# Where a two-layer trunk copies its residual into a bank, takes third chunks' features and spills its residual

## The chip, the cores and the metric

The kernel runs on one core of a Trainium2 chip. The metric is the device time of one launch in microseconds, the median of several runs. A core has five engines that are named in the profile: TensorE (PE, with its weight loads as PEld), VectorE (DVE), ScalarE (ACT), GpSimd (POOL) and SyncE (SP). Each engine takes its own instructions strictly in the order in which the program lists them, so an instruction that waits holds up all that stand behind it on its engine.

## The reference

The reference is a decoder trunk of two layers on 256 tokens of width 2048, in float32. Layer 0 (even) runs two mixers side by side on one input projection; layer 1 (odd) runs an mLSTM. Each layer ends with a gated embedding.

```python
for i in range(DEPTH):                      # DEPTH = 2
    hn = rmsnorm(h, e_norm[j] if i % 2 == 0 else o_norm[j])
    if i % 2 == 0:
        u = hn @ e_w_in[j]                  # HGRN2 and RG-LRU branches
        mix = concatenate([ya, yb]) @ e_w_out[j]
    else:
        u = hn @ o_w_in[j]                  # q, k, v, output gate, z, i and f gates
        mix = yc @ o_w_out[j]               # yc: normalised mLSTM output, gated
    h = h + mix
    pl = rmsnorm(p[i] @ ple_w[i], ple_norm[i])
    h = h + sigmoid(h @ ple_gate_w[i]) * pl
return rmsnorm(h, final_norm)
```

All weights are read once. The residual `h` is what the change's copy and spill are about: 256 tokens by 2048, 2 MB.

## The kernel before

**Numbers in two parts.** A float32 operand is split into a rounded high part and the low rest (`whi`, `wlo` for weights, `ahl` for activations), and a product is three matmuls: high by high, high by low, low by high. A weight tile of 128x1024 (512 KB) lands by SyncE's queue in one of five `raw` buffers. ScalarE casts it to `whi` (L136), VectorE makes `wlo` (L137). Both have four buffers. Two tiles make a *quarter*: 24 matmuls of 128x512 on TensorE (L208 to L210 or L232). So the weights that are cast run at most two quarters ahead of TensorE.

**Stages.** The program is a row of stages, each a product of 256x2048 by 2048x2048 in four output *chunks* of 512 columns: the inputs of layer 0, its output `eo`, the embedding's gate `g0`, queries and keys `oqk`, values `ov`, gates `oog` and `oz`, the output `oo`, the gate `g1`. In a stage, the first two chunks run interleaved (`project_two`): quarters in the order (0,0), (0,1), (1,0), (1,1), (0,2), (1,2), (0,3), (1,3), chunk and quarter. The quarters 2 need the activations that come from the *third* chunk of the stage before.

**Chunks to features.** A stage leaves its chunks token by row; the next stage needs them feature by row. `to_features` transposes blocks on VectorE into a tile `w` (L555), writes it to DRAM and reads it back in four DMAs that rearrange it into a tile `r` (`across`, L674 and L677, all issued by GpSimd), and then waits a number of steps, the *lag*, before it emits the instructions that read `r`: on ScalarE L563 with a gain, L571 without, and splits. The lanes are named `fe`, `fg` and `fo`, and the DRAM tensors `dfe`, `dfg`, `dfo` with the chunk's number. `features` does the same for queries and keys (`dqk`, L1194).

**Order.** Side work is written as Python generators in named lanes. `pump`, called in the middle of each quarter, advances every lane by one step; `drain` runs a lane to its end. A scheduler then orders the instructions of each engine by the program's order and by priorities (`high_priority`); `issue_after` keeps an instruction behind another one in that order.

**Seven products.** The last two chunks of a stage are computed with seven products for eight in a part of the matrix (`seven`). It holds four PSUM banks: A, F and B (`mm`) and E (`mx`). The product A (L232) is made first. ScalarE copies it to F (L335) and its negative to B (L336); then the product on E begins. In the stage `oo` alone, E begins with the residual of chunk 3, copied by ScalarE (L338, `home`), so that the sum needs no extra addition.

**The residual's way.** In layer 0 the residual lies in four tiles `hq` of 512 KB. After stage `g0` the four are written to DRAM (`dh`, L1150, GpSimd's queue), and in stage `oz` four DMAs bring them back (`home`, L1423).

Of the kernel before, what the change touches and what calls it, by code (L numbers as in the profile page):

```python
# [11 lines left out]
F32 = mybir.dt.float32  # L12
# [3 lines left out]
AF = mybir.ActivationFunctionType  # L16
# [3 lines left out]
P = 128  # L20
# [24 lines left out]
def trunk(ctx: ExitStack, tc: tile.TileContext, a, out):  # L45
    nc = tc.nc
    v, s, gp, te, sy = nc.vector, nc.scalar, nc.gpsimd, nc.tensor, nc.sync
# [10 lines left out]
    dr = ctx.enter_context(tc.tile_pool(name="dr", bufs=1, space=bass.MemoryType.DRAM))  # L58
# [4 lines left out]
    last = {}  # L63

    def start(lane, gen):
        lanes.setdefault(lane, []).append(gen)

    def step(lane):
        q = lanes.get(lane)
        while q:  # L70
            if next(q[0], lanes) is not lanes:
                return True
            q.pop(0)
        return False
# [8 lines left out]
    def drain(*which):  # L83
        for lane in which:
            while step(lane):
                pass
# [35 lines left out]
    def block(src, c, n):  # L122
        return src[c * P:(c + n) * P].rearrange("(p n) -> p n", p=P)
# [90 lines left out]
    def split_weights(r):  # L214

        hi, lo = (wp.tile([P, 1024], F32R, name=n, tag=n) for n in ("whi", "wlo"))
        with tc.high_priority(offset=400):
            last["act"] = s.copy(hi, r).ins  # L218
            last["dve"] = v.tensor_tensor(out=lo, in0=r, in1=hi.bitcast(F32), op=ALU.subtract).ins  # L219
        return hi, lo  # L220
# [62 lines left out]
    def seven(w, j, act, qs, kqs, room, part, home=None, order=None):  # L283

        def src(b, side, kq):
            return block(w[4 * (j + b) + kq], side * 1024, 1024)

        def load(tile_of, b, side):
            tiles = []
            for kq in kqs:  # L290
                t = tile_of()
                sy.dma_start(out=t, in_=src(b, side, kq))
                tiles.append(t)
            return tiles

        def ring():
            return wp.tile([P, 1024], F32, name="raw", tag="raw", bufs=5)

        def split(tiles):
            return [split_weights(t) for t in tiles]  # L300

        def add(x, y):
            with tc.high_priority(offset=400):
                for xi, yi in zip(x, y):
                    v.tensor_tensor(out=xi, in0=xi, in1=yi, op=ALU.add)

        def add_loaded(x):
            for xi, kq in zip(x, kqs):
                gp.dma_start(out=xi, in_=src(1, 0, kq), accum_op=ALU.add)

        def soon(out, in0, in1, op):
            with tc.high_priority(offset=450):
                v.tensor_tensor(out=out, in0=in0, in1=in1, op=op)

        def keep(out, bank):
            with tc.high_priority(offset=450):
                s.copy(out, bank)

        def quadrant(side, hf):
            return stationary(act, [2 * kq + side for kq in kqs], hf)  # L320

        def combo(n):
            return [[t for kq in kqs for t in qs[n, kq][x]] for x in range(2)]

        acc = len(kqs) == 2
        rest = [kq for kq in range(4) if kq not in kqs]
        E = px.tile([P, 512], F32, name="mx", tag="mx")
        A, F, B = (pm.tile([P, 512], F32, name="mm", tag="mm") for _ in range(3))
        b5, g = part(), part()
        X = load(room, 0, 0)  # L330
        product(A, quadrant(0, 0), split(X), True)
        if acc:
            add_loaded(X)
        with tc.high_priority(offset=450):
            s.copy(F, A)  # L335
            with tc.issue_after(s.activation(B, F, AF.Copy, scale=-1.0).ins):  # L336
                if home is not None:
                    s.copy(E, home)  # L338
        Y = load(room, 1, 1)
        product(E, combo(4), split(Y), home is None)  # L340
        W = X
        if not acc:
            W = load(ring, 1, 0)
            add(Y, W)
            add(W, X)
        rows = [list(rest), list(rest)]
        did = set()
        for op in order or ORDERS[len(kqs)]:
            if op in "ab":
                b = "ab".index(op)  # L350
                kq = rows[b].pop(0)
                plain(w, j + b, kq, act, ((A, F), (E, B))[b], end=not rows[b])
            elif op == "5":
                product(B, combo(1), split(W))
                add(X, Y)
                if acc:
                    add_loaded(Y)
                keep(b5, B)
            elif op == "6":
                product(B, combo(2), split(X))  # L360
                keep(g, B)
            elif op == "2":
                Z = load(ring, 0, 1)
                product(A, quadrant(1, 0), split(Z))
            elif op == "4":
                product(F, quadrant(1, 1), split(X))
            elif op == "7":
                product(B, combo(3), split(Y))
                soon(b5, B, b5, ALU.subtract)
            elif op == ".":  # L370
                pump()
            elif op == "A":
                yield 0, 0, A
            elif op == "F":
                soon(b5, F, b5, ALU.subtract)
                yield 0, 1, b5
            did.add(op)
            if op in "26" and {"2", "6"} <= did:
                add(X, Z)
        if home is None:  # L380
            soon(g, E, g, ALU.add)
            yield 1, 0, g
        else:
            soon(home, E, g, ALU.add)
            yield 1, 0, None
        yield 1, 1, B
# [163 lines left out]
    def to_features(h, c, act, gain, name, more=None):  # L550

        w = room("w")
        w5 = w.rearrange("p (j c h t) -> p h c j t", j=4, c=4, h=2)
        for hf in range(2):
            v.transpose(w5[:, hf], h[:, hf].rearrange("p (c j q) -> p c j q", c=4, j=4))  # L555
        r = room("r")
        yield from across(w, r, f"d{name}{c}", 6)
        r5 = r.rearrange("p (i c h t) -> p c h i t", i=4, c=4, h=2)
        for b in range(2):
            if gain:  # L560
                x = tp.tile([P, 512], F32, name="xr", tag="hn", bufs=3)
                for k in range(2):
                    s.activation(x[:, k * T:(k + 1) * T].rearrange("p (h i t) -> p h i t", h=2, i=4), r5[:, 2 * b + k],  # L563
                                 AF.Copy, scale=pc(gain, 4 * c + 2 * b + k))
                act[2 * c + b] = split_act(x, "h")
            else:
                hi, lo, both = act_pair()
                for k in range(2):
                    src = r5[:, 2 * b + k]
                    hk, lk = (x[:, k].rearrange("p (h i t) -> p h i t", h=2, i=4) for x in (hi, lo))  # L570
                    s.copy(hk, src)  # L571
                    v.tensor_tensor(out=lk, in0=src, in1=hk.bitcast(F32), op=ALU.subtract)
                act[2 * c + b] = (hi, lo, both)
        if more is not None:
            yield
            more(c, r5)
# [94 lines left out]
    def across(w, r, name, lag):  # L671

        d = dr.tile([P, 1024], F32, name=name)
        gp.dma_start(out=d, in_=w)  # L674
        to = r.rearrange("p (i n) -> p i n", i=4)
        for j in range(4):
            last["hop"] = gp.dma_start(out=to[32 * j:32 * j + 32],  # L677
                                       in_=d.rearrange("(i q) (j n) -> j q i n", i=4, j=4)[j]).ins
        for _ in range(lag):
            yield  # L680
# [413 lines left out]
    hq = []  # L1094
# [27 lines left out]
    act = out_proj(hq, mixed(), "fe")  # L1122
# [22 lines left out]

    acth = ple_gate(hq, two_and_seven(a["g0"], act, ready(act, "fe"), (e0, "q4", 2), in_e0), pls, rp0, hss0, "on", "fg", gate_sums)
    away = []
    for c in range(4):
        d = dr.tile([P, 2, 512], F32, name=f"dh{c}")
        gp.dma_start(out=d, in_=hq[c])  # L1150
        away.append(d)
    l0.close()


# [18 lines left out]
    with tc.tile_pool(name="m1", bufs=2) as m1:  # L1173
# [191 lines left out]
                start("mix", mix_norm())  # L1365
        y = {}
        held = []
        drain("combos")
        store_of = [hp.tile([P, 1024], F32, name="pr", tag="h") for _ in range(2)]
        turn = []  # L1370

# [31 lines left out]
        for jj in (0, 2):  # L1403
            us = [m1.tile([P, 2, 512], F32, name="u", tag="vt", bufs=6) for _ in range(2)]
            for b, hf, src in pair(a["oz"], jj, True):
# [3 lines left out]
                for i in range(2):  # L1409
                    c = hf * 8 + 2 * j + i  # L1410
# [5 lines left out]
        hq = []  # L1416
# [47 lines left out]
        act = out_proj(hq, two_and_seven(a["oo"], y, ready(y, "fm"), (m1, "vt", 6), in_m1, lambda: hq[3][:, 0]), "fo")  # L1464
# [67 lines left out]
        y, yh, t, r = (tp.tile([P, 1], F32, name=n, tag=n, bufs=2) for n in ("fy", "fyh", "ft", "fr"))  # L1532
# [22 lines left out]
        yh, t, r = (tp.tile([P, 1], F32, name=n, tag=n, bufs=2) for n in ("fyh", "ft", "fr"))  # L1555
# [131 lines left out]
```

## Time and profile before

| | us |
|---|---|
| median of three runs (1029.83 to 1030.67) | 1030.06 |
| the profiled execution | 1031.47 |
| span of the profiled execution, first to last instruction | 1029.7 |
| TensorE busy | 1014.8 |
| VectorE busy | 824.3 |
| ScalarE busy | 648.6 |
| GpSimd busy | 105.1 |

The mean granted TensorE clock was 0.995 of the full one. In the rows of a timeline stand the start and the length in us, the engine, the line, the operation, out<-in, the size and the count; in brackets the idle time of the engine before it, and what ended it. A row of waits gives who waited for whom, the sum in us, how often, and the longest. A DMA's row gives the tensor, the count, the size of each and the median time from issue to landing. Busy matmuls overlap: one is shown as 0.39 us long although the next starts 0.23 us later.

### The profile page before, as it was taken

Reading aid. Unit: us, or ns where it says so; the run is one execution under the profiler, and the core shown is the slowest. Engines: PE = TensorE matmul, PEld = TensorE weight load, DVE = VectorE, ACT = ScalarE, POOL = GpSimd, SP = SyncE. Lnnn points to the kernel's source line nnn. Section 1 sums busy time; section 2 is a strip of 40 time slices with the busy share of each in tenths; the row PEclk is TensorE's granted clock in tenths of the full one; section 3 lists DMA queues with packets and bytes.
Section 4 is the critical chain, followed back from the end, with each engine's and each line's share of the span. In section 5 each row is a group of like instructions: output and inputs, shape, how many; then the busy total and the mean of one; then the engine's idle time right before and its main releaser. Section 6 shows DMA issues by size and latency. Waiting matters only on the chain.

```text
span 1029.7 us, 14491 instructions
## 1 busy us (share of the span) xinstructions
PE 1014.8 (99%) x5170; PEld 842.2 (82%) x5170; DVE 824.3 (80%) x1208; ACT 648.6 (63%) x933; POOL 105.1 (10%) x190
## 2 busy tenths in 40 slices
PE   9999999999999999999999999999999999899996
PEld 7888888888888888888788888888888888788886
DVE  6867969969686888887659997778889997886684
ACT  7675554686874555565547866765667767454562
POOL 0111101011111112021011100000011111102000
PEclk9999999999999999999999999999999999999998
DMA  9887756567789799587797755377879899669652
GB/s 360 314 235 240 225 176 197 167 200 224 244 254 305 246 302 290 180 288 261 224 289 249 226 187 192 123 242 203 266 185 285 223 284 330 204 207 287 225 184 82
DMA packets 69672, 242.14 MB, mean 235 GB/s; under 512 B 9024, under 2 KB 10432, under 8 KB 69600
## 3 DMA queue, kind: packets, MB, share of 16 engines
q1 hardware_dynamic: 54720, 193.36, 56.8%
q0 software_dynamic: 14448, 47.33, 16.7%
q8 instruction: 40, 0.66, 0.3%
q10 hardware_dynamic: 432, 0.52, 0.1%
q14 instruction: 32, 0.26, 0.1%
HBM read 221.26 MB, written 19.92 MB: 234 GB/s over the span
## 4 chain that ended last, share of the span: by engine, by line
PE 94%; DMA 2%; issue 2%; ACT 1%; POOL 0%; DVE 0%; ACTq 0%; POOLq 0%
PE mm L232 21%; PE mm L208 17%; PE mm L209 17%; PE mm L210 17%; PE mx L232 5%; PE mx L209 3%; PE mx L210 3%; PE mx L208 3%; PE mm L506 1%; PE mx L506 1%; PE nu L1321 1%; DMA r<-dfg 1%; PE mm L1512 1%; PE mm L1511 1%; PE mm L1513 1%
## 5 line engine op out<-in xcount | busy, mean ns | idle before, releaser
L137 DVE TENSOR_TENSOR wlo<-raw,whi 128x1024 fp32r<-128x1024 f32 (+1 forms) x317 | 381.5, 1214 | 125.8 <-ACT whi L136 118.1
L136 ACT CAST whi<-raw 128x1024 fp32r<-128x1024 f32 (+1 forms) x317 | 330.3, 1046 | 226.6 <-PE mm L210 112.9
L208 PE MATMUL mm<-whi,ahl 128*128 128x512 f32 x768 | 300.3, 391 | 0.0
L209 PE MATMUL mm<-wlo,ahl 128*128 128x512 f32 x768 | 299.0, 389 | 0.0
L210 PE MATMUL mm<-whi,ahl 128*128 128x512 f32 x768 | 298.9, 389 | 0.0
L232 PE MATMUL mm<-whi,ahl 128*128 128x512 f32 x552 | 177.5, 389 | 0.0
L208 PEld LDWEIGHTS mm<-whi,ahl 128*128 128x128 f32 x768 | 144.2, 188 | 30.3 <-issue 0.4
L210 PEld LDWEIGHTS mm<-whi,ahl 128*128 128x128 f32 x768 | 144.1, 188 | 30.3
L209 PEld LDWEIGHTS mm<-wlo,ahl 128*128 128x128 f32 x768 | 144.2, 188 | 29.1
L232 PEld LDWEIGHTS mm<-whi,ahl 128*128 128x128 f32 x552 | 103.6, 188 | 21.6
L232 PE MATMUL mm<-wlo,ahl 128*128 128x512 f32 x276 | 107.4, 389 | 0.0
L219 DVE TENSOR_TENSOR wlo<-ch,whi 128x1024 fp32r<-128x1024 f32 x56 | 67.6, 1221 | 10.9 <-ACT whi L218 9.5
L218 ACT CAST whi<-ch 128x1024 fp32r<-128x1024 f32 x56 | 58.4, 1049 | 16.8 <-PE mm L232 9.3
L208 PE MATMUL mx<-whi,ahl 128*128 128x512 f32 x160 | 62.9, 393 | 1.0 <-ACT whi L136 1.0
L209 PE MATMUL mx<-wlo,ahl 128*128 128x512 f32 x160 | 63.1, 394 | 0.8 <-DVE wlo L137 0.8
L210 PE MATMUL mx<-whi,ahl 128*128 128x512 f32 x160 | 62.9, 393 | 0.0
L232 PEld LDWEIGHTS mm<-wlo,ahl 128*128 128x128 f32 x276 | 51.8, 188 | 10.8
L232 PE MATMUL mx<-whi,ahl 128*128 128x512 f32 x144 | 47.5, 390 | 0.0
L232 PE MATMUL mm<-whi,q 128*128 128x512 f32 x120 | 40.5, 390 | 0.0
L208 PEld LDWEIGHTS mx<-whi,ahl 128*128 128x128 f32 x160 | 30.4, 190 | 7.9 <-ACT whi L136 1.4
L209 PEld LDWEIGHTS mx<-wlo,ahl 128*128 128x128 f32 x160 | 30.3, 189 | 7.4 <-DVE wlo L137 1.1
L210 PEld LDWEIGHTS mx<-whi,ahl 128*128 128x128 f32 x160 | 30.5, 190 | 6.4
(377 smaller groups left out, 1231.9 us busy)
## 6 DMA issues: line engine op xcount, KB each, us to landing
raw<-in_ew_dram SPq DMA_DIRECT2D x64, 512.0 KB, 5.1
raw<-in_g_dram SPq DMA_DIRECT2D x62, 512.0 KB, 4.5
raw<-in_oqk_dram SPq DMA_DIRECT2D x32, 512.0 KB, 5.0
raw<-in_ov_dram SPq DMA_DIRECT2D x32, 512.0 KB, 4.2
raw<-in_eo_dram SPq DMA_DIRECT2D x30, 512.0 KB, 4.9
raw<-in_oo_dram SPq DMA_DIRECT2D x30, 512.0 KB, 5.3
raw<-in_oog_dram SPq DMA_DIRECT2D x24, 512.0 KB, 4.3
raw<-in_oz_dram SPq DMA_DIRECT2D x20, 512.0 KB, 5.1
```

The costliest lines, as they stand in the source:

```text
L136: last["act"] = s.copy(h, r).ins
L137: last["dve"] = v.tensor_tensor(out=l, in0=r, in1=h.bitcast(F32), op=ALU.subtract).ins
L208: te.matmul(ps[hf], xh, wh, start=(k == 0), stop=False)
L209: te.matmul(ps[hf], xh, wl, start=False, stop=False)
L210: last["pe"] = te.matmul(ps[hf], xl, wh, start=False, stop=(k == KT - 1)).ins
L218: last["act"] = s.copy(hi, r).ins
L219: last["dve"] = v.tensor_tensor(out=lo, in0=r, in1=hi.bitcast(F32), op=ALU.subtract).ins
L232: last["pe"] = te.matmul(o, x, y, start=(first and k + i == 0), stop=(end and k == n - 1 and i == 2), skip_group_check=True).ins
L506: last["pe"] = te.matmul(ps[hf][:, o:o + w_], tokens(pact[x], k, hf), (hi, lo)[y][:, k * 512 + o:k * 512 + o + w_], start=(n == mine[0]), ...
L1321: te.matmul(ps[:, 0:n], x[:, i, o:o + P], y[:, b, i], start=(b == 0 and x is sh and y is vh), stop=(b == hf and y is vl))
L1511: te.matmul(o, xh, wh, start=(k == 0), stop=False)
L1512: te.matmul(o, xh, wl, start=False, stop=False)
```

## The change

Three edits. First, in `seven`, the copy of the residual into E is written ahead of the copy of A, behind the last cast of weights that was recorded (`last["act"]`), and no longer behind the negated copy of F. Second, `to_features` waits seven steps instead of six for chunk 2, the third, in all three lanes. Third, the four DMAs of the spill become a lane of their own, which starts after stage `g0`, lets eight steps pass and then issues one DMA a step; the lane is drained ahead of the gates' stage. What is computed stays the same.

```diff
@@ seven
         with tc.high_priority(offset=450):
+            if home is not None:
+                with tc.issue_after(last["act"]):
+                    s.copy(E, home)
             s.copy(F, A)
-            with tc.issue_after(s.activation(B, F, AF.Copy, scale=-1.0).ins):
-                if home is not None:
-                    s.copy(E, home)
+            s.activation(B, F, AF.Copy, scale=-1.0)
@@ to_features
-        yield from across(w, r, f"d{name}{c}", 6)
+        yield from across(w, r, f"d{name}{c}", 7 if c == 2 else 6)
@@ after ple_gate
     away = []
-    for c in range(4):
-        d = dr.tile([P, 2, 512], F32, name=f"dh{c}")
-        gp.dma_start(out=d, in_=hq[c])
-        away.append(d)
+
+    def spill(hq):
+        for _ in range(8):
+            yield
+        for c in range(4):
+            d = dr.tile([P, 2, 512], F32, name=f"dh{c}")
+            gp.dma_start(out=d, in_=hq[c])
+            away.append(d)
+            yield
+
+    start("spill", spill(hq))
@@ behind the values' stage
-        drain("combos")
+        drain("combos", "spill")
```

Lines behind the edits have higher numbers in the changed kernel (L338 becomes L337, L335 and L336 become L338 and L339, L563 becomes L564, L1150 becomes L1155, L1194 becomes L1202).

ScalarE at the head of the seven products of stage `oo`; `mm` are A, F and B, `mx` is E, `ch` and `raw` are weights. Before:

```order
L218 CAST whi<-ch 128x1024 x2
L136 CAST whi<-raw 128x1024 x2
L335 COPY mm<-mm 128x512
L218 CAST whi<-raw 128x1024
L336 ACTIVATE mm<-mm 128x512
L338 COPY mx<-hq 128x512
```

Now:

```order
L218 CAST whi<-ch 128x1024
L337 COPY mx<-hq 128x512
L218 CAST whi<-ch 128x1024
L136 CAST whi<-raw 128x1024 x2
L338 COPY mm<-mm 128x512
L218 CAST whi<-raw 128x1024
L339 ACTIVATE mm<-mm 128x512
```

The copy of the residual stands five instructions earlier, between the casts of the first two tiles of weights.

ScalarE where stage `oqk` begins; `xr<-r` is the third chunk's features, `hq` and `sq` sums of squares of the fourth. Before:

```order
L436 ACTIVATE sq,hss_237<-hq 128x512
L136 CAST whi<-raw 128x1024
L563 ACTIVATE xr<-r,prm 128x256 x3
L150 CAST ahl<-xr 128x2x256
L563 ACTIVATE xr<-r,prm 128x256
L150 CAST ahl<-xr 128x2x256
L136 CAST whi<-raw 128x1024 x6
```

Now:

```order
L437 ACTIVATE sq,hss_237<-hq 128x512
L136 CAST whi<-raw 128x1024 x3
L564 ACTIVATE xr<-r,prm 128x256 x3
L150 CAST ahl<-xr 128x2x256
L564 ACTIVATE xr<-r,prm 128x256
L150 CAST ahl<-xr 128x2x256
L136 CAST whi<-raw 128x1024 x4
```

Two casts of weights, one quarter, now stand ahead of the features. The same pair of casts goes ahead of the third chunk's features in stages `g0` and `g1` (L571, now L572).

GpSimd's queue from the features of stage `g0` to the third chunk of queries and keys. Before:

```order
L1150 DMA dh_4551<-hq 128x1024
L674 DMA dfg_4097<-w 128x1024
L677 DMA r<-dfg_4097 32x4x256 x4
L674 DMA dfg_4155<-w 128x1024
L1150 DMA dh_4553<-hq 128x1024
L677 DMA r<-dfg_4155 32x4x256 x4
L1150 DMA dh_4555<-hq 128x1024
L674 DMA dfg_4438<-w 128x1024
L677 DMA r<-dfg_4438 32x4x256 x4
L674 DMA dfg_4541<-w 128x1024
L1150 DMA dh_4557<-hq 128x1024
L677 DMA r<-dfg_4541 32x4x256 x4
```

Now, from the fourth chunk's features on:

```order
L675 DMA dfg_4541<-w 128x1024
L678 DMA r<-dfg_4541 32x4x256 x4
L675 DMA dqk_4882<-w 128x1024
L678 DMA r<-dqk_4882 32x4x256 x4
L675 DMA dqk_4931<-w 128x1024
L678 DMA r<-dqk_4931 32x4x256 x4
L1155 DMA dh_4963<-hq 128x1024
L1155 DMA dh_5001<-hq 128x1024
L1155 DMA dh_5039<-hq 128x1024
L1155 DMA dh_5077<-hq 128x1024
L675 DMA dqk_5098<-w 128x1024
```

The four writes of the residual left the places among the features' DMAs and stand together between the second and the third chunk of queries and keys.

## The prediction

> **What bounds the kernel now.** I read the page first, then the waits of TensorE, then the stretches around those waits. The page's first part:
>
> ```profile
> PE 1014.8 (99%) x5170; PEld 842.2 (82%) x5170; DVE 824.3 (80%) x1208; ACT 648.6 (63%) x933; POOL 105.1 (10%) x190
> ```
>
> TensorE is busy 1014.8 of 1029.7 us, so an edit that moves no matmul can gain only idle time of TensorE and time at a lower clock. The view of waits, cut to TensorE, says whom it waited for:
>
> ```profile
> PE mx L232 <- ACT mx L338: 2.6, 1, 2.6
> ```
>
> That row, the longest, is one wait of 2.6 us for the residual's copy into its bank, the line that the change moves. Two shorter ones are one place, the second quarter of the second chunk of queries and keys, and stand in the timeline below. The remaining idle time lies ahead of the first matmuls and behind the last, and the change touches neither. The timeline of TensorE at the two places, and the windows of 3.41 us around them (length, busy time of PE, PEld, DVE, ACT, POOL; granted clock; DMA share; GB/s):
>
> ```profile
> 490.91 0.39 PE L210 MATMUL mx<-whi,ahl 128*128 128x512 f32 x1
> 492.32 0.50 PE L208 MATMUL mx<-whi,ahl 128*128 128x512 f32 x1 [1.02 <-ACT whi L136]
> 493.58 0.50 PE L209 MATMUL mx<-wlo,ahl 128*128 128x512 f32 x1 [0.76 <-DVE wlo L137]
> ...
> 500.56 0.39 PE L208 MATMUL mm<-whi,ahl 128*128 128x512 f32 x1
> ```
> ```profile
> 490.94:494.35 3.41, 1.63 (x6) 0.86 (x5) 3.09 (x7) 3.41 (x5) 2.15 (x4) 1.00 0.62 179
> 494.35:497.77 3.42, 3.42 (x9) 2.63 (x8) 3.29 (x9) 0.76 (x1) 0.00 (x0) 0.50 0.86 232
> 497.77:501.18 3.41, 3.41 (x16) 2.79 (x15) 1.39 (x2) 1.47 (x2) 0.00 (x0) 1.00 0.86 294
> 886.88:890.29 3.41, 2.38 (x11) 1.64 (x9) 3.41 (x5) 2.80 (x4) 0.48 (x2) 1.00 0.39 156
> 890.30:893.71 3.41, 1.85 (x8) 1.54 (x9) 3.41 (x4) 1.67 (x4) 1.78 (x4) 1.00 0.77 222
> ```
> ```profile
> 888.87 0.39 PE L232 MATMUL mm<-whi,ahl 128*128 128x512 f32 x1
> 891.86 0.50 PE L232 MATMUL mx<-whi,q 128*128 128x512 f32 x1 [2.61 <-ACT mx L338]
> ...
> 893.36 0.40 PE L232 MATMUL mm<-whi,ahl 128*128 128x512 f32 x1
> ```
>
> Where TensorE waits for nothing, the chain of waits gives its pace:
>
> ```profile
> 348.32 21.76 PE mm L232 x96
> ```
>
> That is 0.2267 us a matmul. At the first place, a quarter of 24 matmuls should follow the one at 490.91 and end 5.44 us after 491.14, at 496.58; the next quarter starts at 500.56. **Lost there: 3.98 us.** Idle time is 1.78 of it. The clock of 0.50 behind it, 9 matmuls in a window that holds 16, is 7 x 0.2267 = 1.6; the rest is the pipeline starting again. At the second place seven matmuls from 888.87 should take 1.59 us and took 4.49. **Lost there: 2.90 us**, at full clock.
>
> **The residual's copy.** ScalarE's timeline shows why the second place waits:
>
> ```profile
> 881.13 1.05 ACT L218 CAST whi<-ch 128x1024 fp32r<-128x1024 f32 x1 [3.02 <-PE mm L210]
> 882.49 1.05 ACT L218 CAST whi<-ch 128x1024 fp32r<-128x1024 f32 x1 [0.31 <-PE mm L210]
> ...
> 889.29 0.57 ACT L335 COPY mm<-mm 128x512 f32<-128x512 f32 x1 [0.30 <-PE mm L232]
> ...
> 890.72 0.59 ACT L336 ACTIVATE mm<-mm 128x512 f32<-128x512 f32 x1
> 891.24 0.57 ACT L338 COPY mx<-hq 128x512 f32<-128x512 f32 x1
> ```
>
> The copy stands behind two copies that need TensorE's product A, done at 889.3. In the new order it stands between the casts of 881.13 and 882.49. It then needs only the residual's landing and a free bank. The landing, from the residual's tile and GpSimd's timeline:
>
> ```profile
> DMA to landing us min/median/max: 5.4/13.9/16.8
> ```
> ```profile
> 852.70 1.05 POOL L1423 DMA_DIRECT2D hq<-dh  x2 [0.39 <-DMA r<-ducn]
> ```
>
> The last is issued at about 853.2 and is there by 853.2 + 16.8 = 870.0, 12 us ahead of the new place. The copy of 0.57 goes into a gap of 0.31, so the cast behind it moves some 0.2 us; its weights are wanted at 889.10, when the gap is long over. With the copy gone from its old place, what is late next at 889.10? The product on E can start; the product on A behind it would start at 889.10 + 1.36 = 890.46. It needs A copied out (889.29 + 0.57 = 889.86) and the low halves of its weights:
>
> ```profile
> 888.87 2.35 DVE L137 TENSOR_TENSOR wlo<-raw,whi 128x1024 fp32r<-128x1024 f32 x2
> ```
>
> They are ready at about 890.1 and 891.2, and wanted at 890.7 and 892.1. The negated copy of F is done at 891.31, and F is written from 893.18. All are early by 0.6 us or more, so I take the whole 2.90; the bounds are 2.90 and, if one of these is late by what it now hides, 2.3.
>
> **The third chunk's features.** ScalarE and GpSimd's timelines at the first place:
>
> ```profile
> 481.42 1.04 ACT L136 CAST whi<-raw 128x1024 fp32r<-128x1024 f32 x1
> 488.44 1.31 ACT L563 ACTIVATE xr<-r,prm 128x256 f32<-128x256 f32 x3 [5.98 <-DMA r<-dfg]
> ...
> 491.23 3.88 ACT L136 CAST whi<-raw 128x1024 fp32r<-128x1024 f32 x4
> ```
> ```profile
> 471.10 0.56 POOL L1150 DMA_DIRECT2D dh<-hq  x1 [14.36 <-DVE hq L607]
> 471.84 0.56 POOL L674 DMA_DIRECT2D dfg<-w  x1 [0.19 <-issue]
> 478.41 2.21 POOL L677 DMA_DIRECT2D r<-dfg  x4 [6.01 <-DMA dfg<-w]
> 481.74 0.56 POOL L674 DMA_DIRECT2D dfg<-w  x1 [1.12 <-DVE hss L430]
> 482.29 0.56 POOL L1150 DMA_DIRECT2D dh<-hq  x1
> ```
>
> ScalarE stands 5.98 us at the features' first instruction, waiting for the rearranging DMA. Behind it stand the two casts that TensorE wants at 491.14. The change puts those two casts ahead. They are then bound by their buffers: four of each kind hold two quarters, so they wait for the quarter that ends at 491.14 - 5.44 = 485.70. Its first half is used up six matmuls earlier, at 484.34. The two casts are made at 484.4 and 485.8, done at 486.9. TensorE runs on to 496.58. The features now start at 486.9 or at the landing, 488.3 if that stays. They take 491.23 - 488.44 = 2.8 us, the next cast 1.05 and its low half 1.24: ready at 493.5, wanted at 496.8. So 3.2 us are left over, without any help from the spill. The whole 3.98 goes, and the lower clock with it.
>
> The same step is made for the third chunk in two other stages, where features took no wait. There four casts go behind a pair of casts for weights, into gaps that the next such cast shows (the first two rows are the earlier stage, the last the later one):
>
> ```profile
> 394.59 1.32 ACT L571 CAST ahl<-r 128x256 fp32r<-128x256 f32 x4
> ...
> 402.76 1.05 ACT L136 CAST whi<-raw 128x1024 fp32r<-128x1024 f32 x1 [2.98 <-PE mx L210]
> ...
> 948.20 1.05 ACT L136 CAST whi<-raw 128x1024 fp32r<-128x1024 f32 x1 [3.02 <-PE mx L210]
> ```
>
> 1.32 us of work in 3 us of idle, a quarter ahead of the use: nothing. Without that cover it would cost at most the 1.32.
>
> **The spill.** Four DMAs of 512 KB leave the queue in which the features' DMAs run. dh at 482.29 shared the engines with the reads that ended at 488.3; without it the landing is between 488.3 and, by the later chunks' median below, 480.1 + 4.7 = 484.8. That only widens the 3.2 us. The four now stand behind the second chunk's reads of queries and keys and ahead of the third's write. They have no wait of their own left, so they go out at once, in the 5.67 us in which GpSimd is idle ahead of that write now:
>
> ```profile
> 549.44 0.56 POOL L674 DMA_DIRECT2D dqk<-w  x1 [5.67 <-DVE w L1181]
> 556.09 2.18 POOL L677 DMA_DIRECT2D r<-dqk  x4 [6.09 <-DMA dqk<-w]
> ```
> ```profile
> DMA to landing us min/median/max: 3.3/4.7/7.6
> ```
> ```profile
> 568.85 0.70 ACT L1194 COPY xr<-r 128x256 f32<-128x256 f32 x2
> 569.45 1.10 ACT L1195 ACTIVATE qk<-xr,prm 128x256 f32<-128x256 f32 x2
> ```
>
> The reads land near 562 to 564 and ScalarE takes them at 568.85, without a wait: some 5 us of cover. The nearest row for a burst beside the weights is the way back, four loads of the same size with two rows of gains around 850 to 870. There the weights took longer to land, by the DMA view of 848 to 872, and TensorE's waits have no row for that stretch:
>
> ```profile
> raw<-in_oo_dram SPq DMA_DIRECT2D x8, 512.0 KB, 8.3
> ```
> So the spill costs nothing while the cover holds; ScalarE may wait a microsecond or two for the third chunk. Uncovered, it costs what the slow rival below works out.
>
> **Sum**: 2.90 + 3.98 = 6.88 us off the span of 1029.7, which gives 1022.8. The profiled execution took 1031.47, 1.8 more than its span; the runs shown have a median of 1030.06, so I take the same off that: **1023.2 us**.
>
> [...]
>
> **Rivals.** (1) *The stall moves on one quarter.* If the features' DMA lands more than 3.2 us later than now, the next pair of casts is late. For: that DMA's last read took 8 us (480.1 to 488.3), on busy engines, and the new order starts two loads of weights earlier. Against: 1 MB less in its queue. With the stall whole again, 1030.06 - 2.90 = 1027.2; halved, about 1025. (2) *The lower clock is not the stall's.* If the 3.4 us at 0.50 came from something else, they stay: 1023.2 + 1.6 = 1024.8. Against: it began right behind the idle window. [...] (3) *The copy gains nothing*, because the product on E finds something else late, or the copy is scheduled as before: 1030.06 - 3.98 = 1026.1. Against: the new order on ScalarE and the times above. (4) *Slower: the spill holds up the third chunk of queries and keys.* All four sit ahead of its write. In the first place 5.98 us of blocking and 2.8 of work cost TensorE 1.8 idle, so ScalarE can be late by about 7.0; at L1194 the work is 1.8, so 5.2 of blocking is free, behind 5 us of cover. A landing late by X costs X - 10.2, and 1.6 for the clock. In today's times the four go out from 543.8 (549.44 - 5.67) to 546.0. If the last takes the 16.8 us of the way back and the write runs only behind it, for the 6.1 it takes now (to 556), it lands at 568.9: X is 13, 4.4 lost, 1027.6. From X = 15.5 the gain is gone; from 17.5 it is slower, and at 20 it is 1023.2 + 9.8 + 1.6 = 1034.6. For: queue order. Against: queues shared the engines around 850 without any wait of TensorE.
>
> **Chances.** Forecast 0.78; (1) 0.07; (2) 0.02; (3) 0.04; (4) 0.09, of which 0.04 ends within 0.2% and 0.05 slower. A difference under 0.2% (2.06 us) can't be told from none here. So faster 0.91, same 0.04, slower 0.05. The forecast's own range is 1022.5 to 1024.2; rivals (1) to (3) reach 1027.2, and the range 1022.5 to 1027.2 leaves out little but (4).
>
> **What would show it.** Right: no wait of TensorE for the copy into mx; the features' xr behind two more casts, and any wait of ScalarE there under 2 us; clock 1.00 around 490; TensorE's waits in sum only the head's. Wrong: TensorE waiting for whi L136 at the quarter after, a clock of 0.50 anywhere before the tail, or ScalarE waiting for r<-dqk by more than 5 us near 565.

## The result and the profile after

The changed kernel takes **1023.5 us** (median of six runs, 1022.66 to 1025.56), beside 1029.94 for the kernel before in six runs (1027.33 to 1031.89): ratio 0.9945, 95% interval 0.9926 to 0.9963. The forecast was 1023.2. The profiled execution took 1022.66, its span 1020.9 instead of 1029.7.

The first part of the page, and the whole view of TensorE's waits, after:

```profile
PE 1010.9 (99%) x5170; PEld 840.2 (82%) x5170; DVE 823.8 (81%) x1208; ACT 649.5 (64%) x933; POOL 105.0 (10%) x190
```
```profile
PE st L98 <- PEq L1686: 0.8, 1, 0.8
```

The one wait left is the program's start. The row of 2.6 us for the copy into `mx` is gone, and so are the two short ones near 490.

ScalarE at the first place, and then GpSimd ahead of it. Rows of a timeline: start, length, engine, line, operation, in brackets the idle time before and its releaser.

```profile
483.52 1.06 ACT L136 CAST whi<-raw 128x1024 fp32r<-128x1024 f32 x1 [0.30 <-PE mm L210]
484.47 1.31 ACT L564 ACTIVATE xr<-r,prm 128x256 f32<-128x256 f32 x3
...
486.73 0.62 ACT L150 CAST ahl<-xr 128x512 fp32r<-128x512 f32 x1
487.60 1.06 ACT L136 CAST whi<-raw 128x1024 fp32r<-128x1024 f32 x1 [0.25 <-PE mx L210]
```
```profile
469.20 0.56 POOL L675 DMA_DIRECT2D dfg<-w  x1 [14.11 <-DVE w L556]
472.92 2.18 POOL L678 DMA_DIRECT2D r<-dfg  x4 [3.17 <-DMA dfg<-w]
```

The features start straight behind a cast, with no wait for `r<-dfg` (5.98 us before). That DMA's write now takes 3.17 us until its reads can be issued; before it was 6.01.

The same matmul can be followed through two executions, since both issue the same 5170 in the same order. By their start times this execution is ahead by 2.4 us at 14 us of the program, by 6.4 behind 490, by 9.25 behind the product on E, and gives 0.4 back at the tail. So 3.98 came from the first place and 2.89 from the second; the 2.4 come from the head, which the change does not touch. (There the profile of before has a wait of 0.95 us at 6.33, after which eight matmuls took 2.93 us; the same eight took 1.83 in e1 and 1.81 in e5 below, so the head is not the same from one execution to the next either.) The windows of TensorE's clock at the first place are full (second figure: TensorE busy; the column behind POOL: granted clock):

```profile
487.41:490.82 3.41, 3.41 (x17) 2.83 (x16) 3.08 (x5) 2.11 (x2) 0.00 (x0) 1.00 1.00 250
490.82:494.24 3.42, 3.42 (x17) 2.84 (x16) 0.57 (x2) 1.05 (x1) 0.00 (x0) 1.00 0.98 335
```

The second place, ScalarE, then TensorE:

```profile
874.77 1.05 ACT L218 CAST whi<-ch 128x1024 fp32r<-128x1024 f32 x1 [3.02 <-PE mm L210]
875.72 0.58 ACT L337 COPY mx<-hq 128x512 f32<-128x512 f32 x1
876.24 1.04 ACT L218 CAST whi<-ch 128x1024 fp32r<-128x1024 f32 x1
```
```profile
882.50 0.40 PE L232 MATMUL mm<-whi,ahl 128*128 128x512 f32 x1
882.74 0.40 PE L232 MATMUL mx<-whi,q 128*128 128x512 f32 x1
...
884.13 0.39 PE L232 MATMUL mm<-whi,ahl 128*128 128x512 f32 x1
```

The copy stands in the gap between two casts, 0.31 us before, and pushes the second by 0.1 us (1.47 us between the starts of the casts instead of 1.36). The product on E follows the one on A after 0.24 us instead of 2.99 (888.87 to 891.86).

The spill, from GpSimd's timeline, and ScalarE where it takes the third chunk of queries and keys:

```profile
533.98 1.63 POOL L1155 DMA_DIRECT2D dh<-hq  x3
537.39 0.54 POOL L1155 DMA_DIRECT2D dh<-hq  x1 [1.78 <-DMA r<-dqk]
543.07 0.53 POOL L675 DMA_DIRECT2D dqk<-w  x1 [5.14 <-DVE w L1189]
550.89 2.22 POOL L678 DMA_DIRECT2D r<-dqk  x4 [7.29 <-DMA dqk<-w]
```
```profile
562.48 0.70 ACT L1202 COPY xr<-r 128x256 f32<-128x256 f32 x2
```

The write of `dqk` waits 7.29 us (6.09 before), the last read lands at 559.36, and ScalarE takes it at 562.48 without a wait: 3.1 us of cover are left of 5.4 (landed 563.42, taken 568.85).

### The profile page after: what moved, and what is told of

The parts are those of the page before. It is cut to its first block, busy times and chain, and to the rows that moved or that the text cites. A ratio compares the mean times of both kernels' runs of the same rounds, so it can differ in the third digit from the quotient of the medians.

```text
span 1020.9 us, 14490 instructions
## 1 busy us (share of the span) xinstructions
PE 1010.9 (99%) x5170; PEld 840.2 (82%) x5170; DVE 823.8 (81%) x1208; ACT 649.5 (64%) x933; POOL 105.0 (10%) x190
## 4 chain that ended last, share of the span: by engine, by line
PE 99%; ACT 0%; DVE 0%; ACTq 0%; issue 0%
PE mm L232 22%; PE mm L208 17%; PE mm L209 17%; PE mm L210 17%; PE mx L232 6%; PE mx L210 4%; PE mx L208 4%; PE mx L209 4%; PE mm L507 1%; PE mx L507 1%; PE nu L1329 1%; PE mm L1520 1%; PE mm L1519 1%; PE mm L1521 1%; PE mx L825 0%; PE st L98 0%
## 5 line engine op out<-in xcount | busy, mean ns | idle before, releaser
L218 ACT CAST whi<-ch 128x1024 fp32r<-128x1024 f32 x56 | 58.5, 1050 | 16.6 <-PE mm L232 9.6
```

## The experiments

Three edits give three kernels with one edit and two with two; then the kernel before once more, the spill made heavier twice, and a last comparison of the whole change with the same without its lag. Medians are in us; "gain" is the median of before times one minus the ratio, with its interval.

**e1: the copy alone.**

```diff
         with tc.high_priority(offset=450):
+            if home is not None:
+                with tc.issue_after(last["act"]):
+                    s.copy(E, home)
             s.copy(F, A)
-            with tc.issue_after(s.activation(B, F, AF.Copy, scale=-1.0).ins):
-                if home is not None:
-                    s.copy(E, home)
+            s.activation(B, F, AF.Copy, scale=-1.0)
```

> The residual's copy is moved, lag and spill stay as before. Theory (two separate stalls that add up): the wait of TensorE for the copy into mx is gone and the product on A follows 1.36 us after the product on E, which takes 2.90 us out of the stream of matmuls; the stall at the second chunk of queries and keys stays with 1 to 2 us idle for whi and wlo and about 3.4 us at a clock of 0.50. Time near 1030 - 2.9 = 1027. Rival (the copy's wait is replaced by another, for the copy of A or the low halves): gain under 1.5 us and a new wait of TensorE in the same place.

Measured: 1025.97 (four runs, 1024.82 to 1026.31), ratio 0.9963 (0.9948 to 0.9978), gain 3.8 (2.3 to 5.4). The three longest waits of TensorE in its profile, then ScalarE's two rows that name the DMA:

```profile
PE st L1143 <- DMA r<-dfg: 1.1, 1, 1.1
PE st L98 <- PEq L1679: 0.8, 1, 0.8
PE mx L209 <- DVE wlo L137: 0.8, 1, 0.8
```
```profile
462.85 0.51 ACT L564 ACTIVATE xr<-r,prm 128x256 f32<-128x256 f32 x1 [5.00 <-DMA r<-dfg]
...
487.36 1.31 ACT L564 ACTIVATE xr<-r,prm 128x256 f32<-128x256 f32 x3 [4.48 <-DMA r<-dfg]
```

The wait for the copy is gone without the other edits. But lag and spill stand here as before, and yet the place near 490 shows a single wait of 0.8 us and no lower clock. And there is a second place that the prediction did not name: TensorE waits 1.1 us near 463 in the embedding's gate sums (L1142 before, L1143 here), sixteen small matmuls that read the second chunk's features directly.

**e2: the lag alone.**

```diff
-        yield from across(w, r, f"d{name}{c}", 6)
+        yield from across(w, r, f"d{name}{c}", 7 if c == 2 else 6)
```

> Only the third chunk's features are taken one step later; copy and spill stay as before. Theory: the two casts ahead of the features are enough without any help from the spill: no wait of TensorE near 490, no clock of 0.50 there, 3.98 us out of the stream; ScalarE still waits for the features' DMA, by 1.5 us or less; the wait of 2.6 us for the copy into mx stays. Time near 1026. Rival (the spill's DMAs among the features' are the cause): ScalarE waits for 3 us or more behind the casts and a part of the stall shows one quarter later; gain under 2 us.

Measured: 1028.49 (ten runs, 1027.20 to 1029.96), ratio 0.9994 (0.9984 to 1.0003), gain 0.6 (-0.3 to 1.6). A miss: the lag by itself cannot be told from no change. TensorE's waits:

```profile
PE mx L232 <- ACT mx L338: 2.6, 1, 2.6
...
PE st L1142 <- DMA r<-dfg: 0.3, 1, 0.3
```

There is no wait near 490 any more, so the lag does what it says. At 463 this execution loses 1.0 us against the first profile of before, and the lag can do nothing about it: it moves only the third chunk.

**e3: the spill alone.** The spill becomes the lane of the change, drained ahead of the gates' stage; copy and lag as before.

```diff
+    def spill(hq):
+        for _ in range(8):
+            yield
         for c in range(4):
             ...
+            yield
+
+    start("spill", spill(hq))
...
-        drain("combos")
+        drain("combos", "spill")
```

> Only the spill is moved; lag 6 and the copy stay as before. Theory (the landing alone decides): with 1 MB less in the queue the reads land as in the changed kernel's trace, where the last was there 4.9 us after the four were issued and about when ScalarE reaches the place with lag 6; so ScalarE waits under 2 us, the casts are in time, the stall and the 0.50 are gone, 3.98 us out of the stream, time near 1026. That makes lag and spill two cures for one stall. Rival (the spill does nothing, as the prediction's sum has it for lag 7): ScalarE still waits 4 to 6 us, the stall stays, time 1030.

Measured: 1027.76 (ten runs, 1025.65 to 1029.77), ratio 0.9983 (0.9971 to 0.9996), gain 1.7 (0.4 to 3.0). Its profile has no wait at 463 or 490; the features of the third chunk start behind a cast, six steps of lag or not. ScalarE, then the windows at the second place:

```profile
479.26 1.30 ACT L563 ACTIVATE xr<-r,prm 128x256 f32<-128x256 f32 x3
```
```profile
882.08:885.49 3.41, 0.84 (x4) 0.37 (x2) 3.41 (x4) 3.09 (x5) 1.97 (x4) 1.00 0.30 62
885.50:888.91 3.41, 3.38 (x8) 2.71 (x9) 2.93 (x5) 0.42 (x1) 0.23 (x1) 0.50 0.94 247
```

So the spill is a second cure of the stall at 490, and of the three edits the only one that bears on 463. Here the 2.6 us wait for the copy is followed by a clock of 0.50, which it was not in the prediction's profile: the place lost 4.4 us instead of 2.9.

**e4: spill and copy, without the lag.** The edits of e1 and e3.

> Spill and copy are moved, the lag stays 6 everywhere. Theory: as in the changed kernel, 6.88 us out of the stream, time near 1023.5, no wait of TensorE between head and tail. Rival (the lag is needed): 2.9 us out, the stall near 490 stays whole or in part, time 1025 to 1027.

Measured: 1022.96 (four runs, 1022.35 to 1023.06), ratio 0.9934 (0.9919 to 0.9949), gain 6.8 (5.2 to 8.3). Between the head and the tail TensorE waits for nothing: the lag is not needed beside the spill.

**e5: the kernel before once more,** to see whether its profile is the same each time.

> The kernel before, profiled once more, to see how much of the 3.98 us that the prediction took from one execution is typical. Theory (the stall is a race between the features' DMA and TensorE, and the clock's window falls as it may): the wait for the copy into mx is 2.6 us again; the idle time near 490 lies anywhere from 0.5 to 2.5 us, with or without a stretch at 0.50 behind it, and a wait of TensorE for the features' DMA of up to 1 us may stand near 463. Rival (the 3.98 is fixed): 1.8 us idle near 490 and 3.4 us at 0.50 behind it, as in the first profile, and no wait near 463.

Measured: 1030.41, one run. TensorE's waits, and the windows at the second place:

```profile
PE mx L232 <- ACT mx L338: 2.6, 1, 2.6
PE st L1142 <- DMA r<-dfg: 1.3, 1, 1.3
...
PE mx L209 <- DVE wlo L137: 0.7, 1, 0.7
```
```profile
885.64:889.05 3.41, 0.80 (x5) 0.34 (x3) 3.41 (x4) 2.98 (x5) 2.08 (x4) 1.00 0.27 54
889.05:892.47 3.42, 3.42 (x8) 2.70 (x9) 2.84 (x5) 0.57 (x1) 0.15 (x1) 0.50 0.96 258
```

The same program, and the loss sits elsewhere: 1.3 us of wait at 463 where the first profile had none, 0.7 near 490 where it had 1.78, and the lower clock behind the copy and not behind 490.

**e6: lag and copy, the spill at its old place.** The edits of e1 and e2.

> The changed kernel with the spill at its old place, among the features' DMAs. Theory from the first runs: the lag cures the place near 490 but not the one near 463, where TensorE's gate sums wait for the second chunk's reads behind the spill's second DMA; so 0.3 to 1.1 us are lost there in most executions, and the time is 1 us or so above the changed kernel: 1024 to 1025.5. Rival (the spill's place is worth nothing beside the lag, as the prediction had it): the same time as the changed kernel, 1023.5, and no wait of TensorE between head and tail.

Measured: 1024.75 (ten runs, 1022.93 to 1026.93), ratio 0.9962 (0.9949 to 0.9976), gain 3.9 (2.5 to 5.2), no more than the copy alone. Its profiled execution, the fastest of the ten, has no wait of TensorE between head and tail, so what the other nine lost, and where, is not shown. The row of the second chunk's features:

```profile
458.45 0.51 ACT L564 ACTIVATE xr<-r,prm 128x256 f32<-128x256 f32 x1 [0.86 <-DMA r<-dfg]
```

With the spill at its old place these features came at 458.45 here, and at 462.42, 462.85, 463.68 and 462.78 in the profiles of before, e1, e2 and e5. TensorE's gate sums ask for them between 461 and 463. From issue to landing, the last of the four DMAs that read these features back took 6.2 to 7.3 us in before, e1, e2 and e5, 4.8 to 5.5 in all seven profiles with the spill moved, and 4.9 in e6. So the spill at its old place makes these reads slower in four of five executions, and not in each.

From the starts of the same matmuls, against the profile after, the us lost at the three places:

| profile | near 463 | near 490 | product on E |
|---|---|---|---|
| before, the prediction's | 0 | 4.0 | 2.9 |
| e5, before again | 2.1 | 0.9 | 4.5 |
| e1, copy | 1.9 | 1.0 | 0 |
| e2, lag | 1.0 | 0 | 2.9 |
| e3, spill | 0 | 0 | 4.4 |
| e4, e6, e9, e10 | 0 to 0.2 | 0 | 0 |

Each place has its edit, but the size at each place is not fixed. The sums of the two profiles of before are close, 6.9 and 7.5. e1 and e5 were through the head 1.7 and 1.9 us sooner than the first profile of before, and lost about as much at 463.

**e7 and e8: the spill twice and three times.** In the whole change each of the four spills is followed by one more write, or two more, of the same 512 KB to places that nothing reads.

```diff
             gp.dma_start(out=d, in_=hq[c])
             away.append(d)
+            for n in range(2):                  # e7: one
+                d2 = dr.tile([P, 2, 512], F32, name=f"dx{n}{c}")
+                gp.dma_start(out=d2, in_=hq[c])
             yield
```

> The changed kernel, with each of the spill's four DMAs issued twice, the second time to a place in DRAM that nothing reads: 4 MB for 2 at the spill's new place. By the fourth rival's sum: the added 2 MB take 10 to 13 us of the queue, so the third chunk's features of queries and keys land 8 to 13 us later; 3.1 us of that is cover (landed 559.4, taken 562.5 in the changed kernel), ScalarE waits 5 to 10 us, of which 5.2 is free; TensorE loses 0 to 5 us, with 1.6 more if the clock drops. Rival (the queue shares the engines and the write passes the spill): features at most 4 us later, ScalarE waits 1 us or less, TensorE nothing, time 1023.5.

> The same with each of the spill's DMAs issued three times, 6 MB for 2, the added ones to places that nothing reads. By the fourth rival's sum: the features of the third chunk land 18 to 27 us later, ScalarE waits 15 to 24 us, TensorE loses 10 us or more near 565 and the time is above 1032, slower than before. Rival (the write passes the spill, or the weights' loads feel it first): ScalarE's wait stays under 5 us and the time under 1026, or TensorE waits for weights ahead of 560.

Measured: 1026.13 and 1032.6, one run each, beside a median of before of 1029.3 (1025.78 to 1031.38). GpSimd's timeline rows for the third chunk's write and reads, ScalarE's row for taking it, and TensorE's wait behind it, of e7:

```profile
543.39 0.53 POOL L675 DMA_DIRECT2D dqk<-w  x1 [3.04 <-DVE w L1191]
560.22 2.23 POOL L678 DMA_DIRECT2D r<-dqk  x4 [16.30 <-DMA dqk<-w]
```
```profile
567.48 0.72 ACT L1204 COPY xr<-r 128x256 f32<-128x256 f32 x2 [4.56 <-DMA r<-dqk]
```
```profile
586.48 0.50 PE L209 MATMUL mm<-wlo,ahl 128*128 128x512 f32 x1 [1.24 <-DVE wlo L137]
```

The same rows of e8, and its windows there:

```profile
549.43 0.53 POOL L675 DMA_DIRECT2D dqk<-w  x1 [2.19 <-DVE qk L1209]
570.06 2.22 POOL L678 DMA_DIRECT2D r<-dqk  x4 [20.09 <-DMA dqk<-w]
```
```profile
574.89 0.71 ACT L1205 COPY xr<-r 128x256 f32<-128x256 f32 x2 [8.61 <-DMA r<-dqk]
```
```profile
576.59 0.51 PE L208 MATMUL mm<-whi,ahl 128*128 128x512 f32 x1 [3.00 <-ACT whi L136]
```
```profile
574.57:577.98 3.41, 0.63 (x2) 0.31 (x3) 1.41 (x2) 3.09 (x7) 1.66 (x4) 1.00 0.18 67
577.98:581.39 3.41, 3.41 (x9) 2.64 (x10) 3.35 (x9) 3.28 (x6) 0.65 (x2) 0.50 0.92 280
```

The reads could be issued at 550.89, 560.22 and 570.06 with 2, 4 and 6 MB of spill ahead: 9.3 and 9.8 us for each 2 MB more, 2.4 us for 512 KB. The write kept its place behind what its queue was given before it: in e7 the eight writes of the spill and then the features' write land in the order of their issue, 2.3 to 2.5 us apart, from 540.55 to 559.94. By the starts of the same matmuls TensorE lost 3.3 us in e7 and 9.9 in e8, and the one run of e8 is slower than each of the 13 runs of before beside it. Two sizes were expected larger: the last read landed 8 and 15 us later than in the changed kernel, where 8 to 13 and 18 to 27 were expected, and ScalarE waited 4.56 and 8.61 us, for 5 to 10 and 15 to 24.

**e9 and e10: the whole change, and the same without the lag, on one chip.** e10 is the kernel of e4.

> The changed kernel once more, beside the next run on one chip. Theory that the extra step of lag is redundant once the spill has left the first place: 1023.0 to 1023.7, within 1 us of the run without the lag. Theory that the lag still protects the first place in unlucky executions: 1023.5, and the run without it 1 us or more slower. No wait of TensorE between the head and the tail in either case.

> The copy moved and the spill moved, the third chunk's features at their old step. Theory that the lag is redundant: 1022.6 to 1023.6, equal to the whole change within 0.1%. Rival that the lag costs something of its own (four casts pushed behind two others in the stages where the features waited for nothing): 1022.4 to 1023.0 and at least 0.5 us below the whole change. Rival that it still protects: 1024.5 or more, with a wait of TensorE near 490 in the profile.

Measured: 1023.47 (six runs, 1022.93 to 1026.15), ratio 0.9946 (0.9930 to 0.9963); and 1022.72 (six runs, 1022.12 to 1024.13), ratio 0.9933 (0.9920 to 0.9946). Neither profile has a wait of TensorE between head and tail, and their spans are 1021.2 and 1021.3. In these runs the lag protects nothing. Whether it costs something stays open: the medians differ by 0.75 us here and by 0.5 between the result and e4, the runs and the intervals overlap, and no row of the profiles shows a place for it. The kernel without the lag is at least no slower, and simpler.

## Why the prediction was right, and where not

**The copy: right.** 2.90 forecast, 2.89 in the stream. Nothing else was late at the product on E: the low halves that the prediction counted on stand at 882.50 in VectorE's timeline, in step with A. In e3 and e5 the old wait cost 4.4 and 4.5, since a clock of 0.50 followed; the copy alone gained 3.8. The term of 2.90 is thus its lower size, not its only one.

**The first place: the sum held, the term was mis-sized.** 3.98 was lost there in one execution. In e5 and e1, with the same instructions there, it was 0.9 and 1.0. What the prediction's sum left out, 2.1 near 463 and 1.6 of clock at E, stands in its place in e5. So 6.88 came out near the measured gain of 5.7 (3.8 to 7.6) although one of its two terms belonged to one execution. That was in part luck: what the first profile lost at 490 alone, 4.0, e5 lost in three ways, 4.6 in all.

**The spill: the step that failed.** "So 3.2 us are left over, without any help from the spill", and of the spill at 482.29, "That only widens the 3.2 us". The lag does hold by itself (e2: nothing lost near 490). But the prediction looked at one of the four DMAs alone, the one at 482.29, and left out the one in the row above, at 471.10. That one went out 0.7 us ahead of the features' write at 471.84, in the same queue. From issue to landing this write took 5.5 to 6.3 us in all five profiles with the spill there, and 3.2 in all seven without. The reads behind it land at 479.4 instead of 488.3. Of these 8.9 us, 2.6 are an earlier issue of the write (2.4 of them come from the head), 2.8 the shorter write (3.17 us until its reads can be issued instead of 6.01), and 3.4 the reads themselves (the last took 4.9 us instead of 8.3). The reads' part is the one that the prediction had, with 484.8 for 488.3; how much of it is due to the spill at 482.29, and how much to the fourth chunk's write at 481.74, is not shown. The write's part is the one that it left out.

The spill issued at 447.61 stands in the same way ahead of the second chunk's reads (454.52), which the gate sums near 463 wait for; this place had no wait in the profile that was read, and it was costed at nothing. Lag and copy gain 3.9 (2.5 to 5.2), spill and copy 6.8 (5.2 to 8.3): of the two edits aimed at the first place, the one taken for free carries the gain, and the one credited with 3.98 adds nothing beside it. The two intervals only touch, so the size of the spill's share is less sure than its sign.

**The lower clock: right that it goes, wrong about whose it was.** The prediction put 1.6 us down to the stall at 490. In the middle of four executions the granted clock stood at 0.50 for one window of 3.41 us, each time behind a window in which TensorE did little, whichever wait made it so: 0.63 (e8), 0.80 (e5), 0.84 (e3) and 1.63 us of work (before). It did not follow 2.38 and 1.85 (before), nor 2.56 and 1.67 (e2): there the same wait of 2.6 us fell across the border of two windows, and its loss was split. The windows of e2:

```profile
883.90:887.32 3.42, 2.56 (x12) 1.78 (x10) 3.42 (x5) 2.81 (x4) 0.49 (x2) 1.00 0.38 153
887.32:890.73 3.41, 1.67 (x7) 1.41 (x8) 3.41 (x4) 1.69 (x3) 1.97 (x4) 1.00 0.73 201
```

The windows lie on a grid: the granted clock of before starts at 9.66 us and changes at 494.35, 497.77 and 1023.42, which is 142, 143 and 297 times 3.4133 us later; that of the profile after starts at 5.17 and changes at 1015.52, 296 times. So the 1.6 us are a matter of where the wait falls on this grid, and rival (2) was wrongly posed: the clock is neither the stall's own nor independent of it.

**The slow rival: the right mechanism, far off.** It said that a landing late by X costs X - 10.2 and 1.6 for the clock. By the places of TensorE (6.4, 6.0 and 6.2 us earlier there than before) the landing is late by 2.3 in the changed kernel (559.36 against 563.42 - 6.36), by 10.0 in e7 and by 17.5 in e8. The formula gives nothing, nothing and 8.9; measured were nothing, 3.3 and 9.9. In e7 the cover was overstated by about 3 us: TensorE waits 1.24 us for low halves at 586 and 0.8 for the keys at 605 (`khl`), two later places that the formula does not have, and the waits cost more than their length. X was taken as 13 because the last spill was given the 16.8 us of the way back; it took 10.0 (537.39 to 547.35), and three of the four went out by 535.6 while reads of the second chunk were still landing.

**Rivals (1) and (3)** did not happen: ScalarE's next pair of casts after the features (487.60 and 488.96) waits for TensorE and not the reverse, and no copy or low half is late at E.

## What to carry to other kernels

When a wait at one place is a race between a DMA and an engine, one profile gives one draw of it: read a second profile before a loss of 4 us is booked to one place. For a late DMA look first at what was issued ahead of it in its own queue; here moving an early, unhurried transfer out from there cured two waits at once (e3: 0 lost near 463 and near 490), while letting the consumer come a step later cured one (e2: 1.0 lost near 463, 0 near 490). Before paying for a second cure, try the kernel with each alone.

## What the runs showed of the hardware

In GpSimd's queue the third chunk's write of queries and keys landed behind the writes issued ahead of it, and its reads could be issued 9.3 us later with 4 MB ahead than with 2, and 9.8 later with 6 than with 4: 2.3 to 2.5 us for each 512 KB beside the stream of weights. From issue to landing, the 512 KB write at 471 took 3.2 us with nothing put ahead of it and 5.5 to 6.3 with 0.5 MB; the write of queries and keys at 543 to 549 took 4.2 to 6.1 us with nothing, 7.2 to 8.8 with 2 MB, 16.6 with 4 MB and 20.1 with 6 MB. What is ahead has a start there (issued 5.7 to 9.1 us before the write in the changed kernel, 533.98 to 537.39 against 543.07), so the times do not grow by the whole 2.4 us for each 512 KB. And the wait of 2.6 us for the copy cost TensorE 2.9 us in before and e2, where it fell across two windows of 3.41 us, and 4.5 in e5, an execution of the same program as before, and 4.4 in e3, where one window took it and the next stood at 0.50. The border is not sharp in these rows: a clock of 0.50 followed a window with 1.63 us of work (before) and not one with 1.67 (e2), but at the tail of e10 it did not follow one with 1.55 either:

```profile
1010.74:1014.15 3.41, 1.55 (x13) 1.34 (x12) 1.62 (x6) 1.79 (x3) 0.00 (x0) 1.00 0.10 38
1014.15:1017.56 3.41, 0.00 (x0) 0.00 (x0) 2.01 (x8) 1.57 (x4) 0.00 (x0) 1.00 0.39 137
```
